# A tile of its own for one activation, quarter sums one product earlier, the first down page behind the additions, and a sum on VectorE

## The chip, the cores and the metric

The kernel runs on one core of a Trainium2 chip. The metric is the device time of one execution in microseconds (us); the time of a kernel is the median of its runs. The core has TensorE (PE, matmuls, with PEld for its weight loads), VectorE (DVE), ScalarE (ACT), GpSimd (POOL), and SyncE (SP), which here issues most of the DMAs.

## The reference

One layer of a hybrid encoder, for 1024 tokens of width 1024, in float32. Only its last part, the gated feed-forward network, is touched by the change.

```python
h = rmsnorm(x, norm1_g)
q, k, v, f_logit, u = split(h @ w_in)
x = x + concat(forgetting_attention(q, k, v, f_logit), multiscale_pool(u)) @ w_out
h2 = rmsnorm(x, norm2_g)                     # 1024 x 1024
gate, up = h2 @ w_gate, h2 @ w_up            # 1024 x 2816 each
x = x + (silu(gate) * up) @ w_down           # 1024 x 1024
return rmsnorm(x, final_g)
```

## The kernel before

**Precision.** Each float32 operand is split into a high part (rounded copy on ScalarE) and a low part (the difference, on VectorE). One product is three matmuls, high by high, low by high and high by low (`mm3`, lines 161 to 163). The split is `split` (lines 120 and 121). So a "page" of weights is ready for its first two matmuls when ScalarE is done, and for the third (L163) when VectorE is done.

**Gate and up.** The hidden width of 2816 is cut into 11 slices `j` of 256. The products of a slice with h2 are done in Strassen's (Winograd's) form, with seven products of half-size blocks instead of eight: P1 to P7. The blocks of h2 are fixed tiles (b11, b21, b22 and the sums t1 to t4, each with h and l). The weights of slice `j` are loaded as two raw tiles r0 and r1, GpSimd makes four sums of them (s1 to s4, lines 1070 to 1073), and the split of each operand is a page `gu{j}_P..`. The products add up in PSUM banks: c1 for P1, P6, P5 and P3 in turn, c2 for P2, c3 for P7 and P4. `snap` (L1135) copies a bank where its running sum is wanted later.

In slices 1 to 10 the third product, P3, is itself done in seven quarter products Q1 to Q7 (`fine_product`); the operands of h2 for these, sums and differences of quarters of b22, are made once, in slice 1, by the twelve steps of `fine_steps` (wholes at L1188, differences at L1195, splits at L121; the last split overwrites a quarter of b22h and b22l). Its weights come as two pages, P3a and P3b. After each quarter product VectorE adds it to a running sum (L1249); the seven share three PSUM regions (`fineA`, `fineB`, `fineC`), so some wait for such an addition. Slice 0 does P3 as one product.

**Features.** From the banks the four corners h11, h12, h21 and h22 of silu(gate) times up are made (`corner`): sums on VectorE (L1154, L1156) or none for h12 of slice 0 (L1151, L1152), the Silu on ScalarE (L1155), the multiplication on GpSimd (L1157). The value under the Silu lies in the tile `q`, of which there is one. GpSimd forms f1 to f4 of the corners (L1161), and all are written to memory (hsdP) for the down projection.

**Down.** It takes the slices in four groups `b` (2, 3, 3, 3 slices), each again in seven products (`ORDER2`). `down_raw` loads rows of w_down (r_wd), `down_sum` makes the four differences (L1312, tile `sum..`, shared by tag), `down_load` fetches the features back (r_f), and `down_page(i)` splits both into a page d0 to d3. After each product VectorE adds the four banks into rows of x (x2f, L1532), which have been reloaded; `gfb`, the final norm's weight, takes the place of tile `wmask`, in which the quarter operand of Q5 lies.

**What sets the order.** The program is written as a sequence; a scheduler then places the instructions on each engine's queue by its own estimate of when they can run, within what tiles and banks allow. `tc.issue_after(x)` keeps an instruction behind `x`. An engine works its queue strictly in order. The loop over `todo` (from line 1354) issues for each product the page two products ahead, the product, the corners due, and on the last slice the first steps of the down projection: `down_raw` after P1, two sums after P6, two loads after P7, and `down_page(0)` after P3a. `finer` holds the twelve quarter steps, of which three are issued after each product.

Of the kernel before, what the change touches and what calls it, by code (L numbers as in the profile page):

```python
# [45 lines left out]
def tile_kernel(  # L46
# [16 lines left out]
    nc = tc.nc  # L63
# [53 lines left out]
    mark = {}  # L117

    def split(hi, lo, src, eng=nc.vector):
        mark["hi"] = nc.scalar.activation(out=hi, in_=src, func=AF.Copy)  # L120
        return eng.tensor_tensor(out=lo, in0=src, in1=f32(hi), op=ALU.subtract)  # L121
# [789 lines left out]
    def blk_tile(key, shape, dt, name):  # L911
        pl, tag = (vpool, IN_V[key]) if key in IN_V else (blk, key)
        return pl.tile(shape, dt, tag=tag, bufs=1, name=name)
# [145 lines left out]
    def wk_tile(tag, bufs, name):  # L1059
        return wk.tile([P, 512], F32, tag=tag, bufs=bufs, name=name)  # L1060
# [79 lines left out]
    def feature(j, name, key):  # L1140
        t = feats[name] = wk_tile("h", 8, f"{name}_{j}")
        if key:
            spills.append((hsd[key, j], t))
        return t

    def corner(j, name, key, src, to):

        h = feature(j, name, to)
        q = wk_tile("q", 1, f"q{name}_{j}")
        if key is None:  # L1150
            nc.scalar.activation(out=q, in_=banks[src, 0], func=AF.Silu)  # L1151
            nc.vector.tensor_tensor(out=h, in0=banks[src, 1], in1=q, op=ALU.mult)  # L1152
        else:
            nc.vector.tensor_tensor(out=q, in0=banks[src, 0], in1=snaps[j, key, 0], op=ALU.add)  # L1154
            nc.scalar.activation(out=q, in_=q, func=AF.Silu)  # L1155
            nc.vector.tensor_tensor(out=h, in0=banks[src, 1], in1=snaps[j, key, 1], op=ALU.add)  # L1156
            nc.gpsimd.tensor_tensor(out=h, in0=h, in1=q, op=ALU.mult)  # L1157
# [93 lines left out]
    def spill(q=nc.scalar):  # L1251
        while spills:
            d, h = spills.pop(0)
            q.dma_start(out=d, in_=h)
# [53 lines left out]
    def down_sum(b, k):  # L1308
        a0, a1 = dict(P5=("b12", "P1"), P6=("P3", "P5"), P7=("P3", "b12"), P4=("P2", "P6"))[k]
        t = blk_tile(SUMS[k], [P, len(GROUPS[b]), 512], F32, f"sum{k}_{b}")  # L1310
        eng = nc.gpsimd if (b, k) in ((0, "P7"), (0, "P4"), (1, "P5")) else nc.vector
        eng.tensor_tensor(out=t, in0=moving[b, a0], in1=moving[b, a1], op=ALU.subtract)  # L1312
        moving[b, k] = t

# [13 lines left out]
    def down_page(i):  # L1328
        b, k = steps2[i]
        n = len(GROUPS[b])  # L1330
        fh, fl, wh, wl = (blk_tile(t, [P, n, 512], R, f"d{i}_{m}") for m, t in enumerate(PAGES[i % 2]))
        split(wh, wl, moving[b, k])
        split(fh, fl, raw2.pop(i))
        stationary[i] = fh, fl, wh, wl
# [19 lines left out]
    for i, (j, k) in enumerate(todo):  # L1354
        if i + 2 < len(todo):
            next_page(*todo[i + 2])
        if i:
            spill()
        if i == 1:
            product(j, k, 0, (0, 1))  # L1360
            with tc.issue_after(mark["turn", ORDER[-1]].ins):
                product(j, k, 0, (2, 3))
                product(j, k, 1)
        elif i and (k in ("P3a", "P3b") or k == "P4" and j):
            acc = [snaps[j, "sU4", n] for n in range(2)]
            pieces = dict(
                P3a=("Q1", "Q2", "Q7", (0, (0, 1)), (0, (2, 3)), "Q6", "Q4"), P4=((1, (0, 1)), "Q5", (1, (2, 3))),
                P3b=("Q3",),
            )
            for piece in pieces[k]:  # L1370
                with tc.issue_after(mark["mm"].ins):
                    if isinstance(piece, str):
                        fine_product(j, "P3", piece, acc)
                    else:
                        product(j, "P4", *piece)
        elif i:
            for n in range(2):
                product(j, k, n)
        if (j, k) == (NG - 1, "P3b"):
            last_features = lambda j=j, k=k: after(j, k)  # L1380
        else:
            after(j, k)
        if j == NG - 1:
            if k == "P1":
                for par in range(2):
                    down_raw(0, par)
            if k == "P6":
                for key in ("P5", "P6"):
                    down_sum(0, key)
            if k == "P7":  # L1390
                for par in range(2):
                    down_load(par)
            if k == "P3a":
                down_page(0)
        if j == 1 and k == "P2":
            finer += fine_steps("b22")
        for _ in range(min(3, len(finer))):
            finer.pop(0)()
        pages.pop((j, k))
# [10 lines left out]
    for k in ("P7", "P4"):  # L1410
        down_sum(0, k)
# [80 lines left out]
    for i, (b, k) in enumerate(steps2):  # L1492
# [3 lines left out]
        if b and k in ("P1", "P2", "P6"):  # L1496
            with tc.issue_after(added.ins):
                down_sum(b, dict(P1="P6", P2="P7", P6="P4")[k])
# [78 lines left out]
```

## Time and profile before

| | |
|---|---|
| median of 3 runs | 1045.78 us (1044.71 to 1046.29) |
| the profiled execution's own time | 1044.93 us |
| its span | 1043.2 us |
| mean granted TensorE clock | 0.995 |
| busy: PE, DVE, ACT, POOL | 98%, 69%, 45%, 39% of the span |
| matmuls (PE) | 5284 |

The profile is one execution. A row of the timeline gives start and duration in us, engine, line, operation, output and inputs, shape and count; in brackets stands the idle time of that engine just before and what ended it. Buffer numbers are left out of names: `gu_P_l` is the low part of any page. A row of windows gives for a stretch its length, the busy time of PE, PEld, DVE, ACT and POOL, the granted clock (1.00 is full), the DMA engines' busy share and GB/s. A duration of a row includes an overlap of some 0.08 us with the next instruction on the engine, so the step from one start to the next is a little shorter.

### The profile page before, as it was taken

To read this page: it belongs to the slowest core of one execution; us is meant where nothing else is said; L and a number is where in the kernel's file an instruction comes from. 1 tells how busy PE (TensorE), PEld (TensorE's weight loads), DVE (VectorE), ACT (ScalarE), POOL (GpSimd) and SP (SyncE) were. 2 spreads that over 40 slices of the span, in tenths; PEclk is the share of its full clock that TensorE was granted. 3 is DMA by queue.
4 is the path that set the end of the run, shared out by engine and by line. 5 is a ranking of instruction groups with operands and counts; after the bars stand their busy time and mean duration, and the time that the engine had idled before them with its cause. 6 is when DMAs were issued, how large, how long until landed. Compare 5 with 4: busy or idle time off the path is not lost.

```text
span 1043.2 us, 14702 instructions
## 1 busy us (share of the span) xinstructions
PE 1026.5 (98%) x5284; PEld 876.5 (84%) x5284; DVE 715.2 (69%) x1130; ACT 465.9 (45%) x747; POOL 410.6 (39%) x317
## 2 busy tenths in 40 slices
PE   9999999999999999999999999999999999999997
PEld 8988888998888888787888888888888778888885
DVE  7464566675986488776455556546548799888886
ACT  7334355655764266443343333333334343333346
POOL 4450121213444141538548457556658330000045
PEclk9999999999999999999999999999999999999999
DMA  7224425233832242333242233323326665352424
GB/s 249 53 57 138 100 78 123 63 103 85 289 123 90 66 151 71 102 117 115 71 142 102 70 132 112 91 101 111 101 101 242 212 241 172 122 194 99 151 91 162
DMA packets 108249, 130.25 MB, mean 125 GB/s; under 512 B 7368, under 2 KB 70352, under 8 KB 108176
## 3 DMA queue, kind: packets, MB, share of 16 engines
q1 hardware_dynamic: 96544, 108.18, 32.9%
q10 hardware_dynamic: 11072, 19.69, 4.9%
q0 software_dynamic: 560, 1.44, 0.4%
q8 instruction: 42, 0.69, 0.3%
q14 instruction: 31, 0.25, 0.1%
HBM read 86.29 MB, written 33.03 MB: 114 GB/s over the span
## 4 chain that ended last, share of the span: by engine, by line
PE 47%; DVE 5%; DMA 2%; issue 1%; ACT 0%; POOL 0%; POOLq 0%; ACTq 0%; DVEq 0%; SPq 0%
PE gu_P L162 9%; PE gu_P L161 9%; PE gu_P L163 9%; PE d L162 5%; PE d L163 5%; PE d L161 5%; DVE d L121 2%; DVE x2f_s L1532 1%; DMA x2f_s<-x2d 1%; DVE x2f_r L1532 1%; DMA r_wd<-in_w_down_dram 0%; DVE gu_P3a_l L121 0%; DMA gfb<-in_final_g_dram 0%; DVE s L1213 0%; DVE b22l L121 0%
## 5 line engine op out<-in xcount | busy, mean ns | idle before, releaser
L162 PE MATMUL d<-d,d 128*128 128x512 f32 (+1 forms) x308 | 119.4, 389 | 1.1 <-DVE d L121 1.1
L163 PE MATMUL d<-d,d 128*128 128x512 f32 (+1 forms) x308 | 119.1, 388 | 0.0
L629 POOL TENSOR_SCALAR p<-p,rr 128x128 f32<-128x128 f32 (+3 forms) x64 | 48.6, 763 | 176.0 <-DVE rr L628 138.1
L161 PE MATMUL d<-d,d 128*128 128x512 f32 x308 | 107.8, 388 | 0.0
L120 ACT ACTIVATE d<-r_f 128x1536 fp32r<-128x1536 f32 (+1 forms) x28 | 38.7, 1384 | 113.6 <-PE d L162 113.6
L1157 POOL TENSOR_TENSOR h<-h,qh 128x512 f32<-128x512 f32 x33 | 61.9, 1875 | 54.3 <-ACT qh L1155 29.9
L121 DVE TENSOR_TENSOR gu_P_l<-r,gu_P_h 128x1024 fp32r<-128x1024 f32 x32 | 52.6, 1647 | 31.0 <-ACT gu_P_h L120 31.0
L1070 POOL TENSOR_TENSOR s<-r 128x1024 f32<-128x1024 f32 x10 | 24.0, 2400 | 122.3 <-DMA r<-in_w_up_dram 62.7
L120 ACT ACTIVATE gu_P_h<-r 128x1024 fp32r<-128x1024 f32 x32 | 33.8, 1061 | 84.7 <-issue 40.8
L162 PEld LDWEIGHTS d<-d,d 128*128 128x128 f32 x308 | 57.8, 188 | 14.2 <-DVE d L121 2.3
L161 PEld LDWEIGHTS d<-d,d 128*128 128x128 f32 x308 | 57.8, 188 | 11.9
L163 PEld LDWEIGHTS d<-d,d 128*128 128x128 f32 x308 | 57.8, 188 | 11.9
L1437 POOL TENSOR_SCALAR sse<-sse 128x1 f32<-128x1 f32 x7 | 3.5, 494 | 155.3 <-ACT junk L1433 155.3
L121 DVE TENSOR_TENSOR gu_P_l<-s,gu_P_h 128x1024 fp32r<-128x1024 f32 (+1 forms) x38 | 51.6, 1365 | 18.9 <-ACT gu_P_h L120 18.8
L626 ACT ACTIVATE p<-p,mn 128x128 f32<-128x128 f32 (+3 forms) x64 | 49.4, 772 | 31.6 <-DVE mn L620 28.7
L648 DVE TENSOR_TENSOR tl<-tp,th 128x512 fp32r<-128x512 f32 (+1 forms) x80 | 49.5, 632 | 9.6 <-ACT th L647 8.6
L121 DVE TENSOR_TENSOR d<-r_f,d 128x1536 fp32r<-128x1536 f32 (+1 forms) x28 | 46.8, 1671 | 6.2 <-ACT d L120 6.2
L163 PE MATMUL qk<-hTh,l_qk 128*128 128x512 f32 x128 | 50.7, 396 | 0.0
L161 PE MATMUL qk<-hTh,h_qk 128*128 128x512 f32 x128 | 50.6, 395 | 0.0
L162 PE MATMUL qk<-hTl,h_qk 128*128 128x512 f32 x128 | 50.4, 394 | 0.0
L647 ACT ACTIVATE th<-tp 128x512 fp32r<-128x512 f32 (+1 forms) x80 | 42.5, 550 | 16.7 <-PE tp L643 13.9
L1532 DVE TENSOR_TENSOR x2f_s<-d,x2f_s 128x512 f32<-128x512 f32 x64 | 42.4, 682 | 10.6 <-PE d L163 10.6
(803 smaller groups left out, 3232.1 us busy)
## 6 DMA issues: line engine op xcount, KB each, us to landing
r_f<-hsdP SPq DMA_DIRECT2D x77, 256.0 KB
r_wd<-in_w_down_dram SPq DMA_DIRECT2D x22, 512.0 KB
r<-in_w_gate_dram SPq DMA_DIRECT2D x21, 512.0 KB
r<-in_w_up_dram SPq DMA_DIRECT2D x21, 512.0 KB
hsdP<-f ACTq DMA_DIRECT2D x40, 256.0 KB
s<-hi SPq DMA_DIRECT2D x64, 128.0 KB
hsdP<-h ACTq DMA_DIRECT2D x32, 256.0 KB
x<-in_x_dram SPq DMA_DIRECT2D x8, 512.0 KB
```

The lines of the kernel that those rows point to most:

```text
L120: mark["hi"] = nc.scalar.activation(out=hi, in_=src, func=AF.Copy)
L121: return eng.tensor_tensor(out=lo, in0=src, in1=f32(hi), op=ALU.subtract)
L161: nc.tensor.matmul(ps, lh, rh, start=start, stop=False, **kw)
L162: nc.tensor.matmul(ps, lh, rl, start=False, stop=False, **kw)
L163: mark["mm"] = nc.tensor.matmul(ps, ll, rh, start=False, stop=stop, **kw)
L626: nc.scalar.activation(out=pr[:, :n], in_=pr[:, :n], func=AF.Exp, scale=-1.0, bias=mn, accum_out=rs)
L629: nc.gpsimd.tensor_scalar(out=pr[:, :n], in0=pr[:, :n], scalar1=rr, scalar2=1.0, op0=ALU.mult, op1=ALU.mult)
L647: nc.scalar.activation(out=th[:, :w], in_=tp[:, :w], func=AF.Copy)
L648: nc.vector.tensor_tensor(out=tl[:, :w], in0=tp[:, :w], in1=f32(th[:, :w]), op=ALU.subtract)
L1070: g(out=s1, in0=a21, in1=a22, op=ALU.add)
L1157: nc.gpsimd.tensor_tensor(out=h, in0=h, in1=q, op=ALU.mult)
L1532: added = nc.vector.tensor_tensor(out=row, in0=ps, in1=row, op=ALU.add)
```

## The change

It has four edits. The corner without a running sum (h12 of slice 0) gets tile `e2` instead of `q`; `e2` is the tag of a quarter operand, made later. The twelve quarter steps begin after slice 1's P1 instead of its P2. The first down page is placed behind the addition that came last in the program when it is issued (`mark["add"]`). The difference P5 of the second group moves from GpSimd to VectorE.

```diff
     def corner(j, name, key, src, to):
 
         h = feature(j, name, to)
-        q = wk_tile("q", 1, f"q{name}_{j}")
+        q = wk_tile("q" if key else "e2", 1, f"q{name}_{j}")
         if key is None:
...
     def down_sum(b, k):
         a0, a1 = dict(P5=("b12", "P1"), P6=("P3", "P5"), P7=("P3", "b12"), P4=("P2", "P6"))[k]
         t = blk_tile(SUMS[k], [P, len(GROUPS[b]), 512], F32, f"sum{k}_{b}")
-        eng = nc.gpsimd if (b, k) in ((0, "P7"), (0, "P4"), (1, "P5")) else nc.vector
+        eng = nc.gpsimd if (b, k) in ((0, "P7"), (0, "P4")) else nc.vector
...
             if k == "P3a":
-                down_page(0)
-        if j == 1 and k == "P2":
+                with tc.issue_after(mark["add"].ins):
+                    down_page(0)
+        if j == 1 and k == "P1":
             finer += fine_steps("b22")
```

The scheduler answers these edits with other orders. PE at the beginning of slice 1, before (`gu1_P20` and `gu1_P21` are the two PSUM banks of P2, `gu1_P2_h` and `_l` its page):

```order
L161 MATMUL gu1_P20_5251<-b21h_4435,gu1_P2_h_5172 128x512
L162 MATMUL gu1_P20_5251<-b21l_4436,gu1_P2_h_5172 128x512
L161 MATMUL gu1_P21_5264<-b21h_4435,gu1_P2_h_5172 128x512
L162 MATMUL gu1_P21_5264<-b21l_4436,gu1_P2_h_5172 128x512
L163 MATMUL gu1_P20_5251<-b21h_4435,gu1_P2_l_5173 128x512
```

The same place in the changed kernel:

```order
L161 MATMUL gu1_P10_5217<-b11h_4433,gu1_P1_h_5133 128x512
L162 MATMUL gu1_P10_5217<-b11l_4434,gu1_P1_h_5133 128x512
L161 MATMUL gu1_P11_5230<-b11h_4433,gu1_P1_h_5133 128x512
L162 MATMUL gu1_P11_5230<-b11l_4434,gu1_P1_h_5133 128x512
L161 MATMUL gu1_P20_5261<-b21h_4435,gu1_P2_h_5172 128x512
L162 MATMUL gu1_P20_5261<-b21l_4436,gu1_P2_h_5172 128x512
L161 MATMUL gu1_P21_5274<-b21h_4435,gu1_P2_h_5172 128x512
L162 MATMUL gu1_P21_5274<-b21l_4436,gu1_P2_h_5172 128x512
L163 MATMUL gu1_P10_5217<-b11h_4433,gu1_P1_l_5134 128x512
```

P1 now stands ahead of P2, and eight matmuls instead of four stand ahead of the first that reads a low half. On VectorE the multiplication of h12 (L1152) has moved from behind the splits of P1, P2 and P6 to ahead of them.

VectorE in slice 1, before, from the third quarter difference on (`fine_b22..` are the quarter operands, `qh22` the first sum of corner h22, which reads P7's bank):

```order
L1195 TENSOR_TENSOR fine_b2211_5328<-fine_b2211_5328,fine_b2200_5288 128x512
L121 TENSOR_TENSOR gu1_P3a_l_5333<-s4_1_5095,gu1_P3a_h_5332 128x1024
L121 TENSOR_TENSOR fine1_b22_5283<-fine_b2200_5288,fine1_b22_5283 128x512
L121 TENSOR_TENSOR fine3l_b22_5287<-fine_b2201_5290,fine3h_b22_5286 128x512
L1213 TENSOR_TENSOR s4_1_5095<-s4_1_5095 128x256
L121 TENSOR_TENSOR fine2l_b22_5285<-fine_b2211_5328,fine2h_b22_5284 128x512
L1213 TENSOR_TENSOR s4_1_5095<-s4_1_5095 128x256 x2
L1154 TENSOR_TENSOR qh22_1_5406<-gu1_P70_5339,sn1_sU40_5401 128x512
L121 TENSOR_TENSOR gu1_P4_l_5371<-r1_1_5089,gu1_P4_h_5370 128x1024
L1249 TENSOR_TENSOR sn1_sU40_5401<-fineA_1P3_5432,sn1_sU40_5401 128x256
L121 TENSOR_TENSOR gu1_P3b_l_5420<-s4_1_5095,gu1_P3b_h_5419 128x768
L1156 TENSOR_TENSOR h22_1_5405<-gu1_P71_5352,sn1_sU41_5403 128x512
```

The same stretch in the changed kernel:

```order
L1195 TENSOR_TENSOR fine_b2211_5295<-fine_b2211_5295,fine_b2200_5252 128x512
L121 TENSOR_TENSOR fine3l_b22_5251<-fine_b2201_5254,fine3h_b22_5250 128x512
L1195 TENSOR_TENSOR fine_b2210_5370<-fine_b2210_5370,fine_b2211_5295 128x512
L121 TENSOR_TENSOR gu1_P3a_l_5338<-s4_1_5095,gu1_P3a_h_5337 128x1024
L121 TENSOR_TENSOR fine2l_b22_5249<-fine_b2211_5295,fine2h_b22_5248 128x512
L121 TENSOR_TENSOR b22l_4444<-fine_b2210_5370,b22h_4443 128x2x256
L1213 TENSOR_TENSOR s4_1_5095<-s4_1_5095 128x256 x3
L121 TENSOR_TENSOR gu1_P4_l_5376<-r1_1_5089,gu1_P4_h_5375 128x1024
L1154 TENSOR_TENSOR qh22_1_5411<-gu1_P70_5344,sn1_sU40_5406 128x512
L1249 TENSOR_TENSOR sn1_sU40_5406<-fineA_1P3_5432,sn1_sU40_5406 128x256
L121 TENSOR_TENSOR gu1_P3b_l_5420<-s4_1_5095,gu1_P3b_h_5419 128x768
L1156 TENSOR_TENSOR h22_1_5410<-gu1_P71_5357,sn1_sU41_5408 128x512
```

The fourth whole, its difference and the split of b22l now stand ahead of P4's split and of `qh22`, and these two have changed places.

VectorE in the last slice, before, from P4's split on (`d0_1` and `d0_3` are the low halves of the first down page):

```order
L121 TENSOR_TENSOR gu10_P4_l_8080<-r1_10_7771,gu10_P4_h_8079 128x1024
L121 TENSOR_TENSOR d0_1_8176<-r_f0_8073,d0_0_8175 128x1024
L1154 TENSOR_TENSOR qh22_10_8112<-gu10_P70_8047,sn10_sU40_8107 128x512
L1249 TENSOR_TENSOR sn10_sU40_8107<-fineA_10P3_8125,sn10_sU40_8107 128x256
L121 TENSOR_TENSOR gu10_P3b_l_8121<-s4_10_7818,gu10_P3b_h_8120 128x768
L1156 TENSOR_TENSOR h22_10_8111<-gu10_P71_8060,sn10_sU41_8109 128x512
L1249 TENSOR_TENSOR sn10_sU40_8107<-fineC_10P3_8133,sn10_sU40_8107 128x256
L121 TENSOR_TENSOR d0_3_8178<-r_wd0_0_7963,d0_2_8177 128x1024
L1249 TENSOR_TENSOR sn10_sU41_8109<-fineB_10P3_8141,sn10_sU41_8109 128x256
```

The changed kernel, from the addition that stands last in these rows on:

```order
L1249 TENSOR_TENSOR sn10_sU41_8109<-fineB_10P3_8141,sn10_sU41_8109 128x256
L1249 TENSOR_TENSOR sn10_sU41_8109<-fineA_10P3_8125,sn10_sU41_8109 128x256
L1249 TENSOR_TENSOR sn10_sU41_8109<-fineB_10P3_8141,sn10_sU41_8109 128x256
L121 TENSOR_TENSOR d0_3_8178<-r_wd0_0_7963,d0_2_8177 128x1024
L121 TENSOR_TENSOR d0_1_8176<-r_f0_8073,d0_0_8175 128x1024
L1249 TENSOR_TENSOR sn10_sU41_8109<-fineA_10P3_8125,sn10_sU41_8109 128x256
L1249 TENSOR_TENSOR sn10_sU40_8107<-fineA_10P3_8125,sn10_sU40_8107 128x256
```

Both splits of the page now stand behind five of the slice's seven additions and ahead of the last two.

## The prediction, made before the result was known

> **What bounds the kernel now.** I read the page first. TensorE is busy for all but a sliver, so only work that keeps it waiting, or slows its clock, can move the time.
>
> ```profile
> PE 1026.5 (98%) x5284; PEld 876.5 (84%) x5284; DVE 715.2 (69%) x1130; ACT 465.9 (45%) x747; POOL 410.6 (39%) x317
> ```
>
> Next the view of waits, for PE alone. Its columns are microseconds in all, times, longest. The four rows that matter lie in three places: where slice 1 of the gate and up products begins, in slice 1's quartered third product, and from the end of the last slice into the down projection.
>
> ```profile
> PE gu_P L163 <- DVE gu_P_l L121: 2.3, 1, 2.3
> PE fineB_10P L161 <- DVE sn_sU L1249: 2.1, 1, 2.1
> PE fineB_1P L162 <- DVE b22l L121: 1.7, 1, 1.7
> PE d L162 <- DVE d L121: 1.1, 2, 0.6
> ```
>
> The timeline of PE gives exact idle times (in brackets) and the first matmuls of slices 1, 2 and 3 (435.62, 479.10, 516.88):
>
> ```profile
> 435.62 0.39 PE L161 MATMUL gu_P<-b21h,gu_P_h 128*128 128x512 f32 x1
> 438.96 0.58 PE L163 MATMUL gu_P<-b21h,gu_P_l 128*128 128x512 f32 x1 [2.27 <-DVE gu_P_l L121]
> 474.94 0.39 PE L162 MATMUL fineB_1P<-b22l,gu_P3a_h 128*128 128x256 f32 x1 [1.73 <-DVE b22l L121]
> 479.10 0.39 PE L161 MATMUL gu_P<-b11h,gu_P_h 128*128 128x512 f32 x1
> 516.88 0.39 PE L161 MATMUL gu_P<-b11h,gu_P_h 128*128 128x512 f32 x1
> 817.47 0.38 PE L161 MATMUL fineB_10P<-b22h,gu_P3a_h 128*128 128x256 f32 x1 [2.09 <-DVE sn_sU L1249]
> 824.04 0.39 PE L161 MATMUL d<-d,d 128*128 128x512 f32 x1
> 853.24 0.50 PE L162 MATMUL d<-d,d 128*128 128x512 f32 x1 [0.64 <-DVE d L121]
> ```
>
> An undisturbed slice takes 516.88 − 479.10 = 37.78 (its 144 full and 42 half-wide matmuls are the time of 165, so 0.229 for a full one); slice 1 takes 43.48, so 5.70 is lost there, though its two waits are only 2.27 + 1.73 = 4.00. The rest is the clock. In these stretches the column PEclk (after the five engines) is the granted clock:
>
> ```profile
> 439.00:443.00 4.00, 4.00 (x11) 3.14 (x12) 3.47 (x3) 0.93 (x2) 4.00 (x2) 0.57 0.17 66
> 818.00:822.00 4.00, 4.00 (x17) 3.43 (x17) 0.42 (x1) 0.00 (x0) 0.00 (x0) 0.57 0.65 222
> 473.00:477.00 4.00, 2.27 (x13) 1.83 (x14) 2.79 (x4) 1.06 (x1) 4.00 (x2) 1.00 0.02 7
> ```
>
> After the waits of 2.27 and 2.09 the mean clock over 4 us is 0.57, which costs 4 × 0.43 = 1.7 each; after 1.73 it stays 1.00. So 4.00 + 1.70 = 5.70 closes slice 1. In all 2.27 + 1.7 + 1.73 + 2.09 + 1.7 + 1.1 = **10.6 us** can be won.
>
> The Trainium skill, "TensorE: Matmul & The Clock Gate" (section "What's actually happening"), lets the clock fall to half after an idle window of about 3.4 us; here it fell after 2.1, so the measurement decides. By the page's figure the two clock terms would not belong to the waits; that result is a rival below.
>
> **The activation's own tile (first wait).** One tile `q` serves all corners in turn, so each waits for GpSimd's product of the one before.
>
> ```profile
> 440.46 0.60 ACT L1151 ACTIVATE qh<-gu_P 128x512 f32<-128x512 f32 x1 [3.47 <-POOL h L1157]
> 441.09 0.69 DVE L1152 TENSOR_TENSOR h<-gu_P,qh 128x512 f32<-128x512 f32 x1
> 433.14 5.76 DVE L121 TENSOR_TENSOR gu_P_l<-r,gu_P_h 128x1024 fp32r<-128x1024 f32 x2 [1.85 <-ACT gu_P_h L120]
> ```
>
> Until 441.78 bank c1 (slice 0's P3) isn't free for slice 1's P1, so PE takes P2 (b21) first, whose low half is the second of the two splits at 433.14, done at 438.9. With its own tile the Silu needs only PE's P3, which ends before slice 0's last P4, and the multiplication goes ahead of the two splits. It costs DVE 0.69, which fits into the 1.85 idle before 433.14; on ScalarE the Silu's 0.60 lies in idle time ahead of the next DMA issue. P1 then runs first and P2's high parts are interleaved, so eight matmuls (8 × 0.229 = 1.8) run before the first low half is needed at 437.4. The first split ends at 433.14 + 2.9 = 436.0, the second at 438.9 against a need after 441.9. The term is −2.27 − 1.7 = **−3.97**; if the first split slips past 437.4, the term shrinks one for one (bound: −2.5, both splits needed).
>
> **Quarter sums one product earlier (second wait).** The last of them, b22l, ends at 474.88; PE's wait of 1.73 ended at 474.94, so it was wanted at 473.2.
>
> ```profile
> 449.58 0.69 DVE L1154 TENSOR_TENSOR qh<-gu_P,sn_sP 128x512 f32<-128x512 f32 x1 [1.19 <-POOL h L1157]
> 452.56 2.99 DVE L1188 TENSOR_TENSOR fine_b<-b22h,b22l 128x512 f32<-128x512 f32 x3
> 456.61 2.13 DVE L1195 TENSOR_TENSOR fine_b<-fine_b,fine_b 128x512 f32<-128x512 f32 x3
> 460.39 0.68 DVE L121 TENSOR_TENSOR fine3l_b<-fine_b,fine3h_b 128x512 fp32r<-128x512 f32 x1
> 465.40 1.23 DVE L121 TENSOR_TENSOR gu_P_l<-r,gu_P_h 128x1024 fp32r<-128x1024 f32 x1 [2.12 <-ACT gu_P_h L120]
> 472.80 2.08 DVE L121 TENSOR_TENSOR b22l<-fine_b,b22h 128x512 fp32r<-128x512 f32 x1 [0.70 <-ACT b22h L120]
> 461.93 0.75 DVE L1213 TENSOR_TENSOR s<-s 128x256 f32<-128x256 f32 x2
> 485.74 1.21 DVE L121 TENSOR_TENSOR gu_P_l<-s,gu_P_h 128x1024 fp32r<-128x1024 f32 x1
> 490.73 0.39 PE L161 MATMUL gu_P<-t2h,gu_P_h 128*128 128x512 f32 x1
> 450.00:470.00 20.00, 20.00 (x98) 16.95 (x97) 14.84 (x22) 9.62 (x14) 2.65 (x3) 1.00 0.21 71
> ```
>
> Nothing is added, but all twelve steps now stand ahead of P4's split. What is late next? The qh row at 449.58 waits for GpSimd's product of the corner before, which doesn't move, while PE stands 4 us earlier: five products after 435.62 its first quarter matmul comes near 463.0 (5 × 24 × 0.229), P4 behind three quarter products at 465.1. P4 adds to a bank that DVE's second qh has to read first. So from 449.58 DVE must do two qh and one h (0.6 each in the queue: 1.9), four wholes (4 × 1.0), four differences (2.8), four small splits (2.5), three page splits (3.5) and three short sums (1.1): 15.8, done at 465.4. ScalarE's halves are not waited for if each is ready in turn; GpSimd is busy only 2.65 of these 20 us (last column but three), so I take free durations. The bounds of a new wait are 0 (two wholes run free at 0.6) and 2.1 (each of a dozen hand-overs adds 0.15). P4's split also releases the load of slice 2's second raw tile, from which GpSimd makes the sum for P6: the split's end goes from 466.6 to about 464.8, 1.8 earlier, while PE is 5.7 earlier. P6's split now ends at 486.95, PE wants it two matmuls behind 490.73: a slack of 4.2 falls to 0.3, so nothing more is waited for there. I take 0.5. The term is −1.73 + 0.5 = **−1.2**.
>
> **First down page behind the additions (third wait).**
>
> ```profile
> 809.78 1.22 DVE L121 TENSOR_TENSOR d<-r_f,d 128x1024 fp32r<-128x1024 f32 x1
> 814.84 2.25 DVE L121 TENSOR_TENSOR d<-r_wd,d 128x1024 fp32r<-128x1024 f32 x1
> 817.00 0.41 DVE L1249 TENSOR_TENSOR sn_sU<-fineB_10P,sn_sU 128x256 f32<-128x256 f32 x1
> 822.14 0.42 DVE L1249 TENSOR_TENSOR sn_sU<-fineA_10P,sn_sU 128x256 f32<-128x256 f32 x1 [3.06 <-PE fineA_10P L163]
> ```
>
> The two splits (1.14 and 2.16 in the queue) stand ahead of the addition that PE waits for. Moved behind the fifth addition in the order, that addition ends 3.3 earlier, at 814.1, before PE's need at 817.47 − 2.09 = 815.4. Q4 (six half-wide matmuls, 0.7) and its addition end near 816.5, the two splits at 818.8, in the 3.06 that DVE now idles. What is queued behind them is the addition of Q5, ended by 819.2; PE wants it for Q3 after Q4, half of P4, Q5 and the rest of P4, 4.1 behind 815.4: 819.5. The page itself is needed a Q3 later, near 820.2. The term is −2.09 − 1.7 = **−3.8**; the bound is −2.1, if the splits take 2 us longer beside GpSimd and Q3 waits 1.7.
> SP is reordered too: gfb, which waits for Q5's matmuls (tile `wmask`), goes ahead of two r_f loads of the second group and one x2 row.
>
> ```profile
> 822.14 0.33 SPq L1404 DMA_DIRECT2D gfb<-in_final_g_dram  x1
> ```
>
> It comes 3.8 earlier with Q5, so these three are issued near 818.5; the first of them to be read, the x2 row, has its reader behind three down steps of 24 × 0.229 = 5.5, after 836. I cost it at 0; without that cover it is one load of 512 KB, about 3 us.
>
> **The sum on VectorE (fourth wait).**
>
> ```profile
> 844.01 1.21 DVE L121 TENSOR_TENSOR d<-sumP,d 128x1024 fp32r<-128x1024 f32 x1
> 847.72 4.39 POOL L1312 TENSOR_TENSOR sumP<-r_wd 128x1536 f32<-128x1536 f32 x1 [9.09 <-DVE x2f_s L1532]
> 848.67 4.52 DVE L121 TENSOR_TENSOR d<-sumP,d 128x1024 fp32r<-128x1024 f32 x1
> 865.90 1.74 DVE L1312 TENSOR_TENSOR sumP<-r_wd,sumP 128x1536 f32<-128x1536 f32 x1
> 840.90 1.28 SPq L1304 DMA_DIRECT2D r_wd<-in_w_down_dram  x3
> 840.00:850.00 10.00, 10.00 (x46) 8.29 (x45) 10.00 (x13) 4.02 (x4) 2.28 (x1) 1.00 0.94 347
> ```
>
> DVE is full here (10.00 of 10), and its split beside GpSimd's sum takes 4.52 instead of 1.21. The sum costs 1.74 on DVE, and takes 3.31 away: 1.57 saved, against waits of 0.64 and then 0.45 (the rest of 1.1). The term is **−1.1**. It must find its load landed: 1.5 MB from 840.90 at 347 GB/s ends near 845.4, or 847 beside its neighbour; DVE comes at 848.7, and both move about 4 earlier. Bounds: −1.1, and +1.5 if it waits.
>
> The Trainium skill, "SBUF — State Buffer" (the table whose row is "Run DVE + GpSimd concurrently"), says to schedule whichever is off the critical path, which speaks for leaving the sum on GpSimd. By the rows the split ends 1.1 after GpSimd's sum does, as if it waited for all of it, so the sum charges DVE either way, and 1.74 is the cheaper.
>
> **Sum.** −3.97 − 1.2 − 3.8 − 1.1 = −10.1. The profiled execution took 1044.93 (span 1043.2): 1034.8. It lies 0.85 under the median of 1045.78, from which the same sum gives 1035.7. I forecast **1035.3**.
>
> **Rivals.**
> *The wait comes back in slice 1 or 2.* DVE's hand-overs make P4, or slice 2's P6, 2.1 late instead of 0.5, and the clock halves: 1.6 + 1.7 = 3.3 lost, **1038.6**. For it: 15.8 of work for 15.5 of time. Against it: the one long idle time in DVE's rows there, 2.12, hung on ScalarE, whose own order also moves forward. Chance 0.17.
> *The DVE sum waits for its load, or DVE stays the bound after 830.* Nothing of 1.1 is won and 1.5 is added: **1037.9**. For it: DMA at 0.94. Chance 0.13.
> *The half clock doesn't belong to the waits.* Both stay: 3.4 less, **1038.7**. Against it: 1.00 in the untroubled slices, and both falls begin right behind a wait. The page on the clock gate cited above would give this time. Chance 0.04.
> *The tile doesn't change PE's order in effect*, since both splits are needed anyway: 4.0 less, **1039.3**. Against: each low half is an instruction of its own. Chance 0.05.
> *Slower.* The twelve quarter steps run beside GpSimd and each takes 2.08, like b22l, not 0.68: 12 × 1.4 = 16.8 late, ahead of the pages of P5, P3a and P4; PE loses about 16 + 1.7 against 10.6: **1052**. It decides from about 10 us of lateness, seven of the twelve steps. Against it: GpSimd is busy 2.65 of the 20 us there. Chance 0.04.
>
> **How the numbers follow.** Forecast 0.55; rivals 0.17, 0.13, 0.04, 0.05, 0.04; 0.02 for anything else. The range runs from 1033.8 (all of 10.6, from 1044.93, and 0.5 of scatter) to 1040.0, which takes in four rivals. The likeliest case alone: 1034 to 1037. A measurement of this kernel can tell 0.2% (2.1 us) from nothing: faster 0.91, same 0.04, slower 0.05.
>
> **What would show it.** Right: PE's first matmul of slice 1 reads b11, and no wait over 0.3 follows before slice 2, which starts 37.8 to 38.5 later; the clock is 1.00 from slice 1 to the end of the down projection; DVE's splits of 128x1024 in the down projection all stay near 1.2; down matmuls start about 9 earlier than 824. Wrong: a clock row of 0.57 anywhere there, a PE wait on a P4 or P6 page in slices 1 and 2, or DVE idle ahead of the moved sum with a DMA as releaser.

## The result, and the profile after

The changed kernel takes **1034.55 us** (median of 4 runs, 1034.12 to 1035.78) against 1045.24 for the kernel before, run beside it (4 runs, 1042.77 to 1046.29): a ratio of 0.9903, 95% interval 0.9883 to 0.9923. The prediction was 1035.3, between 1033.8 and 1040.0. Two repeats gave ratios of 0.9909 (0.9892 to 0.9927) and 0.9912 (0.9898 to 0.9925). One run of the kernel before, of 5882 us, was in a slow state and is left out of the first of these. The profiled execution took 1035.78, with a span of 1034.0 against 1043.2.

The page's busy times, and PE's waits of the changed kernel (microseconds in all, times, longest):

```profile
PE 1022.9 (99%) x5284; PEld 873.6 (84%) x5284; DVE 711.6 (69%) x1131; ACT 465.2 (45%) x747; POOL 405.4 (39%) x316
...
PE d L162 <- DVE d L121: 0.5, 1, 0.5
...
PE gu_P L163 <- DVE gu_P_l L121: 0.3, 1, 0.3
```

The waits of 2.3, 2.1 and 1.7 are gone. One of 0.5 is left of the 1.1 in the down projection, and one of 0.3 is new. The timeline of PE shows where (in brackets the idle time just before); the rows are the first matmuls of slices 1, 2 and 3, the new wait, the first down matmul, the old wait, and the last matmul:

```profile
436.82 0.39 PE L161 MATMUL gu_P<-b11h,gu_P_h 128*128 128x512 f32 x1
474.44 0.39 PE L161 MATMUL gu_P<-b11h,gu_P_h 128*128 128x512 f32 x1
481.51 0.50 PE L163 MATMUL gu_P<-b21h,gu_P_l 128*128 128x512 f32 x1 [0.27 <-DVE gu_P_l L121]
512.81 0.39 PE L161 MATMUL gu_P<-b11h,gu_P_h 128*128 128x512 f32 x1
815.76 0.40 PE L161 MATMUL d<-d,d 128*128 128x512 f32 x1
855.05 0.50 PE L162 MATMUL d<-d,d 128*128 128x512 f32 x1 [0.45 <-DVE d L121]
1026.33 0.28 PE L163 MATMUL dlast<-d,d 128*128 128x256 f32 x1
```

The last matmul before was this one:

```profile
1035.50 0.28 PE L163 MATMUL dlast<-d,d 128*128 128x256 f32 x1
```

From these rows and those of the prediction the span divides as follows (us):

| stretch | before | after | difference | predicted |
|---|---|---|---|---|
| start to slice 1 (untouched) | 435.62 | 436.82 | +1.20 | 0 |
| slice 1 | 43.48 | 37.62 | −5.86 | −5.17 (tile, quarter sums) |
| slice 2 to the first down matmul | 344.94 | 341.32 | −3.62 | −3.8 (first down page) |
| first to last down matmul | 211.46 | 210.57 | −0.89 | −1.1 (sum on VectorE) |
| behind it | 7.7 | 7.7 | 0 | 0 |

The first row is scatter: in the eleven profiles of the experiments, which leave this part unchanged too, slice 1 begins anywhere from 435.80 to 437.29. The changed stretches won 10.37 where 10.07 had been forecast. The third row is the sum of two things: slice 2 itself grew from 37.78 to 38.37, where the new wait is, and the rest of the stretch fell from 307.16 to 302.95, by 4.21. In the view by windows (length, the five engines, granted clock, DMA share, GB/s) the two places that had shown 0.57 now show 1.00:

```profile
436.00:440.00 4.00, 4.00 (x20) 3.30 (x19) 4.00 (x2) 1.06 (x1) 4.00 (x2) 1.00 0.00 0
440.00:444.00 4.00, 4.00 (x19) 3.34 (x18) 3.19 (x3) 0.71 (x2) 4.00 (x2) 1.00 0.17 66
814.00:818.00 4.00, 4.00 (x22) 3.40 (x21) 2.82 (x6) 2.75 (x4) 0.00 (x0) 1.00 0.87 231
```

VectorE's timeline shows the four edits at work: the multiplication of h12 ahead of the two splits (432.46), b22l and P4's split in time (462.87, 464.59), the page's two splits behind the fifth addition (811.75 to 813.23), and the sum (841.12):

```profile
432.46 0.68 DVE L1152 TENSOR_TENSOR h<-gu_P,qh 128x512 f32<-128x512 f32 x1
434.54 5.82 DVE L121 TENSOR_TENSOR gu_P_l<-r,gu_P_h 128x1024 fp32r<-128x1024 f32 x2 [1.40 <-ACT gu_P_h L120]
...
462.87 0.68 DVE L121 TENSOR_TENSOR b22l<-fine_b,b22h 128x512 fp32r<-128x512 f32 x1
...
464.59 1.22 DVE L121 TENSOR_TENSOR gu_P_l<-r,gu_P_h 128x1024 fp32r<-128x1024 f32 x1
...
811.75 0.42 DVE L1249 TENSOR_TENSOR sn_sU<-fineB_10P,sn_sU 128x256 f32<-128x256 f32 x1 [0.29 <-PE fineB_10P L163]
812.09 1.22 DVE L121 TENSOR_TENSOR d<-r_wd,d 128x1024 fp32r<-128x1024 f32 x1
813.23 1.22 DVE L121 TENSOR_TENSOR d<-r_f,d 128x1024 fp32r<-128x1024 f32 x1
...
841.12 1.76 DVE L1312 TENSOR_TENSOR sumP<-r_wd 128x1536 f32<-128x1536 f32 x1
```

One sign that the prediction named did not come: not all of VectorE's splits of 128x1024 in the down projection stayed near 1.2. Those at 818.63, 823.87 and 825.90 took 2.32, 2.11 and 2.31, beside GpSimd's last work on the features; PE waited for none of them.

So the sum of the forecast came out. The experiments ask whether its terms did: each edit alone, then the sum's place, then the clock.

### The profile page after: what moved, and what is told of

Its sections match the earlier page's. It is cut to its first block, busy times and chain, and to the rows that moved or that the text cites. A ratio compares the mean times of both kernels' runs of the same rounds, so it can differ in the third digit from the quotient of the medians.

```text
span 1034.0 us, 14701 instructions
## 1 busy us (share of the span) xinstructions
PE 1022.9 (99%) x5284; PEld 873.6 (84%) x5284; DVE 711.6 (69%) x1131; ACT 465.2 (45%) x747; POOL 405.4 (39%) x316
## 4 chain that ended last, share of the span: by engine, by line
PE 49%; DVE 2%; DMA 1%; issue 1%; POOL 1%; ACT 0%; SPq 0%; POOLq 0%; ACTq 0%; DVEq 0%
PE gu_P L163 9%; PE gu_P L162 9%; PE gu_P L161 9%; PE d L162 5%; PE d L163 5%; PE d L161 5%; DMA r_wd<-in_w_down_dram 1%; DVE d L121 1%; DVE x2f_s L1533 0%; DMA r<-in_w_up_dram 0%; POOL f L1161 0%; DMA hsdP<-f 0%; DVE gu_P_l L121 0%; POOL h L1157 0%; POOL hsdP L1254 0%
## 5 line engine op out<-in xcount | busy, mean ns | idle before, releaser
L1157 POOL TENSOR_TENSOR h<-h,qh 128x512 f32<-128x512 f32 x33 | 64.5, 1955 | 34.8 <-ACT qh L1155 26.9
L1155 ACT ACTIVATE qh<-qh 128x512 f32<-128x512 f32 x33 | 20.9, 632 | 64.6 <-POOL f L1161 32.6
```

## Experiments: each edit alone

The four kernels ran on one chip beside 24 runs of the kernel before (median 1044.25, from 1042.82 to 1046.98). They had 5, 8, 10 and 10 runs, in the order below. The gains are one minus the ratio, times 1044.25.

**The tile alone.**

```diff
-        q = wk_tile("q", 1, f"q{name}_{j}")
+        q = wk_tile("q" if key else "e2", 1, f"q{name}_{j}")
```

> The tile edit alone, put into the kernel before. Prediction's theory (the first wait belongs to the shared tile, and the half clock to the wait): slice 1 goes from 43.48 to 39.5 us, no wait of 2.27, no clock of 0.57 near its beginning, the wait of 1.73 on b22l stays; time 4.0 below the kernel before (1041.2). Rival, hand-on: VectorE's chain in slice 1 hangs on GpSimd's product at 449.58, which does not move, so b22l ends where it did and PE, 3.97 earlier, waits 5.7 for it instead of 1.73; slice 1 stays at 43.5 and the time at 1045. Between them lies a wait on b22l of 2 to 5 us.

Measured: 1040.8 (ratio 0.9962, 0.9949 to 0.9975), a gain of 3.97, by the interval 2.6 to 5.3. PE's timeline, slice 1's first matmul, the wait on b22l, and slice 2's first:

```profile
436.07 0.39 PE L161 MATMUL gu_P<-b11h,gu_P_h 128*128 128x512 f32 x1
470.78 0.39 PE L162 MATMUL fineB_1P<-b22l,gu_P3a_h 128*128 128x256 f32 x1 [1.62 <-DVE b22l L121]
474.98 0.39 PE L161 MATMUL gu_P<-b11h,gu_P_h 128*128 128x512 f32 x1
```

Slice 1 takes 38.91. The wait on b22l is 1.62, not 5.7: counted from slice 1's first matmul PE wants b22l 4.5 us earlier than before, and VectorE's chain came 4.6 earlier. The hand-on rival falls.

**The quarter steps after P1 alone.**

```diff
-        if j == 1 and k == "P2":
+        if j == 1 and k == "P1":
             finer += fine_steps("b22")
```

> The twelve quarter steps after P1 alone. Prediction's theory: the wait of 1.73 goes and nothing takes its place, since PE is not earlier than in the kernel before; slice 1 goes from 43.48 to 41.75, the wait of 2.27 and its half clock stay; time 1.7 below the kernel before. Rival, contention: the twelve steps beside GpSimd take 2.08 each, not 0.68, and PE waits for pages of P5, P3a or P4; slice 1 longer than 50. Rival, hand-on: P4's split or its bank is late instead, slice 1 stays near 43.5.

Measured: 1039.98 (ratio 0.9965, 0.9954 to 0.9977), a gain of 3.65, twice the 1.7 expected; by the interval it is 2.4 to 4.8. PE's timeline has the first wait, and slice 2 begins 39.77 after slice 1's first matmul at 437.29:

```profile
440.35 0.50 PE L163 MATMUL gu_P<-b21h,gu_P_l 128*128 128x512 f32 x1 [1.99 <-DVE gu_P_l L121]
477.06 0.39 PE L161 MATMUL gu_P<-b11h,gu_P_h 128*128 128x512 f32 x1
```

39.77 is an undisturbed slice and the wait: 37.78 + 1.99. The wait on b22l is gone with nothing in its place, so neither contention nor hand-on happened. But there is no half clock behind the wait of 1.99, although the prediction charged 1.7 to that wait. Why the gain is larger is taken up below, behind the probes of the clock.

**The first down page behind the additions alone.**

```diff
             if k == "P3a":
-                down_page(0)
+                with tc.issue_after(mark["add"].ins):
+                    down_page(0)
```

> The first down page behind the additions alone. Prediction's theory: the wait of 2.09 and the half clock behind it both go; from the first matmul of slice 2 to the first of the down projection 344.94 becomes 341.1 us; time 3.8 below the kernel before. Rival, the half clock does not belong to the wait: a clock of 0.57 over 4 us stays near 818, that stretch takes 342.85 and the time is 2.1 below. Rival, hand-on: the page's splits hold up the addition of Q5, and Q3 waits 1.7; the time is 2.1 below too, but with a wait on fineA at Q3.

Measured: 1040.54 (ratio 0.9967, 0.9957 to 0.9977), a gain of 3.45. Between slice 2 (480.70) and the first down matmul lie 340.72 us, with no wait and no half clock of their own: as expected, and neither rival. Its two other waits, and the clock behind each in windows laid on the places where the clock can change, showed something else:

```profile
439.61 0.50 PE L163 MATMUL gu_P<-b21h,gu_P_l 128*128 128x512 f32 x1 [2.49 <-DVE gu_P_l L121]
474.96 0.39 PE L162 MATMUL fineB_1P<-b22l,gu_P3a_h 128*128 128x256 f32 x1 [2.27 <-DVE b22l L121]
480.70 0.39 PE L161 MATMUL gu_P<-b11h,gu_P_h 128*128 128x512 f32 x1
821.42 0.40 PE L161 MATMUL d<-d,d 128*128 128x512 f32 x1
```

```profile
435.40:438.80 3.40, 1.72 (x8) 1.10 (x6) 3.40 (x2) 1.06 (x1) 3.40 (x2) 1.00 0.01 2
438.80:442.20 3.40, 2.59 (x11) 2.17 (x12) 3.40 (x3) 0.60 (x1) 3.40 (x2) 1.00 0.18 72
442.20:445.60 3.40, 3.40 (x16) 2.81 (x16) 2.46 (x4) 1.70 (x2) 3.32 (x3) 1.00 0.06 17
...
472.90:476.30 3.40, 1.34 (x8) 1.25 (x9) 2.76 (x3) 0.51 (x1) 3.40 (x2) 1.00 0.00 0
476.30:479.70 3.40, 3.40 (x12) 2.95 (x12) 1.78 (x2) 0.55 (x1) 3.40 (x2) 0.50 0.00 0
```

The longer wait, 2.49, left the clock at 1.00; the shorter one, 2.27, halved it. The longer lies across two windows, in which PE is idle for 1.68 and 0.81; the shorter lies nearly whole in one, idle for 2.06 (2.04 on the grid's exact edges).

**The sum on VectorE alone.**

```diff
-        eng = nc.gpsimd if (b, k) in ((0, "P7"), (0, "P4"), (1, "P5")) else nc.vector
+        eng = nc.gpsimd if (b, k) in ((0, "P7"), (0, "P4")) else nc.vector
```

> The sum of the second down group on VectorE alone. Prediction's theory: both waits of the down projection, 0.64 and 0.45, belong to GpSimd's sum and go; from the first down matmul to the last 211.46 becomes 210.4 us, and the split of 4.52 takes 1.2; time 1.1 below. Rival: the second wait belongs to VectorE's full queue at the first page of 128x1536 and stays, as the changed kernel's trace suggests (0.45 there); 210.8, time 0.6 below. Rival: the sum waits for its load of 1.5 MB, VectorE shows idle time ahead of it released by a DMA, nothing won.

Measured: 1043.19 (ratio 0.9991, 0.9981 to 1.0000), a gain of 0.94, by the interval 0 to 2.0. In its profile the down projection has no wait. But neither has it in the profiles of the tile alone and the page alone, where the sum is still GpSimd's. The page alone, GpSimd and then VectorE:

```profile
846.75 4.49 POOL L1312 TENSOR_TENSOR sumP<-r_wd 128x1536 f32<-128x1536 f32 x1 [10.14 <-DVE d L121]
```

```profile
845.51 1.21 DVE L121 TENSOR_TENSOR d<-r_f,d 128x1024 fp32r<-128x1024 f32 x1
846.64 1.21 DVE L121 TENSOR_TENSOR d<-sumP,d 128x1024 fp32r<-128x1024 f32 x1
850.17 2.15 DVE L121 TENSOR_TENSOR d<-r_f,d 128x1024 fp32r<-128x1024 f32 x1
```

Here the split of sumP started at 846.64, 0.11 ahead of GpSimd's sum, and took 1.21. The four additions from PSUM that follow it ran beside the sum undisturbed, from 847.8 to 850.2, and the next split ended at 852.32, 1.08 behind the sum's end. In the kernel before the split started 0.95 behind the sum and took 4.52, ending 1.08 behind it. So a split that starts while GpSimd's sum is running waits for its end; what the sum costs hangs on whether a split or the additions fall beside it. Six profiles of this case have the sum on GpSimd (before, tile alone, steps alone, page alone, and two below), and in all six it starts while a split is running on VectorE and ends 3.43 to 3.46 behind the start of VectorE's next instruction, as if it too had waited for that split. Where the next instruction is another split (four profiles), that split took 4.52 each time; where it is the additions from PSUM (two), they ran on. Which split is running when the sum can start is a matter of about a microsecond; in four of the six the profile names the sum's load as what it had waited for.

PE pays less than VectorE. From its first to its last down matmul it takes 209.71 to 209.85 in the profiles without a wait there (tile, page and sum alone), and 211.46 and 211.47 in the two where the split took 4.52 (before and steps alone).

## Experiments: where the sum belongs

Three kernels took up that question, each measured beside the changed kernel itself: the sum left on GpSimd, the changed kernel as it is, and the sum later on VectorE. The first two ran side by side:

> The changed kernel once more, beside the two below. Theory: waits in VectorE's work vary little from execution to execution, the clock's grid lies elsewhere each time; since no wait of over 1.6 us is left, the clock stays at 1.00 from slice 1 to the last matmul wherever the grid lies, and the time scatters less than that of the kernel before (1042.8 to 1047.0, 24 runs): 1034.1 to 1036. Rival: the scatter of the kernel before has another source, and this one scatters by 4 us too.

> The changed kernel with the sum of the second group left on GpSimd. Prediction's theory: the sum beside VectorE's split costs 1.1 on PE wherever it falls, so this is 0.6 to 1.1 slower than the changed kernel, with a split of 128x1024 of over 4 us and waits of 0.6 on L162. Rival, formed on the four single edits: only a split that starts while GpSimd's sum is running waits for the sum's end; four additions from PSUM do not wait. The load lands near 841.0, the split of sumP starts at 841.0 too and is ahead of the sum or behind it by 0.1 us. If ahead, the additions run beside the sum, the next split takes about 2.1, PE has no wait over 0.3 from 830 to 870 and the time is 0.45 below the changed kernel; if behind, 0.6 above.

```diff
-        eng = nc.gpsimd if (b, k) in ((0, "P7"), (0, "P4")) else nc.vector
+        eng = nc.gpsimd if (b, k) in ((0, "P7"), (0, "P4"), (1, "P5")) else nc.vector
```

Measured: the changed kernel 1035.76 (1035.03 to 1035.91); with the sum on GpSimd 1033.76, its runs being 1036.76, 1033.50, 1033.55 and 1033.97. Three of its four runs lie below every run of the changed kernel, the fourth above them all. So the fourth edit, taken back, mostly makes the other three faster, not slower; the two forecasts, 0.45 below the changed kernel and 0.6 above it, each name the side of one kind of run, and both are too small. The run of 1036.76 is the profiled one. GpSimd's row, VectorE's, and PE's:

```profile
840.23 3.94 POOL L1312 TENSOR_TENSOR sumP<-r_wd 128x1536 f32<-128x1536 f32 x1 [9.54 <-DMA r_wd<-in_w_down_dram]
```

```profile
839.61 1.21 DVE L121 TENSOR_TENSOR d<-r_f,d 128x1024 fp32r<-128x1024 f32 x1
840.74 4.52 DVE L121 TENSOR_TENSOR d<-sumP,d 128x1024 fp32r<-128x1024 f32 x1
```

```profile
845.31 0.50 PE L162 MATMUL d<-d,d 128*128 128x512 f32 x1 [1.42 <-DVE d L121]
```

The sum started while the first split ran; the second started 0.51 behind the sum, and took 4.52. With the sum on VectorE, the repeated profile of the changed kernel shows the other price, a wait for the load in VectorE's queue:

```profile
841.17 1.76 DVE L1312 TENSOR_TENSOR sumP<-r_wd 128x1536 f32<-128x1536 f32 x1 [0.78 <-DMA r_wd<-in_w_down_dram]
```

PE waits 0.69 and 0.49 there. VectorE idle ahead of the moved sum with a DMA as releaser was one of the prediction's signs of being wrong; the first profile of the changed kernel had not shown it. The sum is not read before the next sum (P6 of the second group), some 15 us later, which led to a third place for it:

```diff
+                if (b, k) == (1, "P1"):
+                    down_sum(b, "P5")
                 down_sum(b, dict(P1="P6", P2="P7", P6="P4")[k])
...
-            down_sum(b + 1, "P5")
+            if b:
+                down_sum(b + 1, "P5")
```

> The changed kernel with the second group's sum kept on VectorE but taken later: behind the first page of the second group, just ahead of the sum that reads it, instead of behind the first group's page of P5. Theory (formed on the repeated run): at its place in the changed kernel the sum waits up to 0.8 for its load and then delays two splits, which costs PE 0.45 to 1.2; at the later place its load has long landed, and PE's waits on L162 near 844 and 855 go, without a new one behind 858; the time is 0.5 to 1.2 below the changed kernel, about 1034.6 on the chip where that takes 1035.5, and it scatters less than the sum on GpSimd. Rival: VectorE is full from 815 to 870 and the wait only moves behind 858; no difference.

> The changed kernel again, beside the two others with the second group's sum elsewhere. Theory: 1034.1 to 1036, with the sum waiting 0.1 to 0.8 for its load in the profile and PE 0.4 to 1.2 on L162. Rival: the 2.0 us between this and the sum on GpSimd of the last call was scatter, and the three agree within 0.5 us.

> The changed kernel with the sum on GpSimd, again. Theory of luck: two kinds of execution, as in the last call (1033.5, 1033.6, 1034.0 and 1036.8): where VectorE's split starts ahead of GpSimd's sum, nothing is lost (about 1033.6), where it starts behind, the split takes over 4 us and PE waits 1.9 in all (about 1035.5 to 1036.8). The profile shows one of the two, in agreement with its own time. Rival: it is slower by 1.1 in every execution, as the prediction's term says.

Measured on one chip, beside 9 runs of the kernel before (1044.66):

| | median | runs | ratio to before (95%) |
|---|---|---|---|
| changed kernel | 1035.15 | 1034.43 to 1036.66 | 0.9912 (0.9898 to 0.9925) |
| sum on GpSimd | 1033.98 | 1033.80, 1033.83, 1034.14; 1036.51 | 0.9902 (0.9888 to 0.9916) |
| sum later on VectorE | 1034.03 | 1033.87 to 1034.23 | 0.9897 (0.9884 to 0.9911) |

The runs of the changed kernel and of the late sum do not overlap; the medians lie 1.12 apart. The profiles account for it: from PE's first to its last down matmul are 210.71 in the changed kernel here (the sum waited 0.16 for its load, PE 0.49) and 209.60 with the late sum. In the late sum's profile VectorE waits for no load, and PE has no wait in the down projection:

```profile
851.70 1.75 DVE L121 TENSOR_TENSOR d<-r_wd,d 128x1536 fp32r<-128x1536 f32 x1
853.36 1.88 DVE L1536 TENSOR_TENSOR x2f_r<-d,x2f_r 128x512 f32<-128x512 f32 x3
855.16 1.75 DVE L1312 TENSOR_TENSOR sumP<-r_wd 128x1536 f32<-128x1536 f32 x1
```

Its own theory held, with 1.1 in the forecast 0.5 to 1.2. Its four runs lie within 0.4 us, with the median of the sum on GpSimd and none of the longer runs that has. The sum on GpSimd shows two kinds of execution both times, six near 1033.8 and two near 1036.6, as the theory of luck says. Both profiled ones are of the slower kind; in both the stretch of down matmuls is 212.06 or 212.07, 2.2 to 2.5 longer than in the profiles without a wait there, and so most of the 2.8 that part the two kinds. The faster kind is known here by its time alone. That the profiled run was of the slower kind both times, and none of the six others, leaves another reading open: that taking the profile shifts the load. The profiles of the tile and the page alone, where the sum costs nothing, show that it need not.

Whether the changed kernel scatters less, as its forecast said, is not settled: its thirteen runs lie from 1034.12 to 1036.66, one end outside 1034.1 to 1036, and the 24 of the kernel before from 1042.82 to 1046.98, but few runs spread less than many. Nor do the 24 times go with the granted clock: the five runs with a mean clock of 0.994 took 1043.6 to 1044.4, the four with 0.997 took 1042.8 to 1045.1.

## Experiments: what halves the clock

Two probes put a delay into VectorE's queue ahead of the addition that PE waits for, in slices 2 to 9 of the changed kernel.

```diff
+            if q == "Q7":
+                for _ in range(HOLD.get(j, 0)):
+                    nc.vector.tensor_tensor(out=out, in0=out, in1=out, op=ALU.max)
             mark["add"] = nc.vector.tensor_tensor(out=out, in0=ps, in1=out, op=ALU.add)
```

> The changed kernel with repeated maxima of the running sum with itself (it stays as it is) on VectorE ahead of Q7's addition in slices 2 to 9, 9 to 17 of them, so that PE waits about 1 to 4 us once in each slice. Window theory: the clock is decided on a fixed grid of 3.413 us, and falls to half for one such window behind a window in which PE was idle for more than about half of it (the six traces: 2.04 fell, 1.66 did not); so waits under 1.7 never fall, waits of 2.0 to 3.4 fall only where one window holds enough of them, waits over 3.9 always do. Rival, length: every wait over 2.0 falls, wherever it lies. Rival, whole window: only a window without any matmul falls, so no wait under 3.4 does.

The delays came out far longer than meant: ten of these maxima, which read and write only SBUF, took 13.09 beside GpSimd's sums, so PE waited 11 to 14 us each time. All eight waits halved the clock, on which the three theories agree. The second probe reads PSUM instead, and ten of its operations took 4.54 at the same place (a row of each probe, then the edit):

```profile
555.44 13.09 DVE L1253 TENSOR_TENSOR sn_sU<-sn_sU 128x256 f32<-128x256 f32 x10
```

```profile
546.27 4.54 DVE L1253 SCALAR_TENSOR_TENSOR sn_sU<-fineB_3P,sn_sU 128x256 f32<-128x256 f32 x10
```

```diff
-                    nc.vector.tensor_tensor(out=out, in0=out, in1=out, op=ALU.max)
+                    nc.vector.scalar_tensor_tensor(
+                        out=out, in0=ps, scalar=0.0, in1=out, op0=ALU.mult, op1=ALU.add
+                    )
```

> As the first probe of the clock, but the delay is made of 9 to 16 operations that read Q7's bank, multiply by zero and add the running sum (it stays as it is), so that none of them waits for GpSimd and each takes about 0.35. PE should wait between 1 and 4 us in each of slices 2 to 9. Window theory: half clock exactly behind each window of the 3.413 grid that holds more than 1.75 to 2.04 us of PE's idle time; so waits of 2.1 to 3.4 that lie across a window's edge, with under 1.75 on each side, leave the clock at 1.00. Length theory: every wait above 2.0 brings it. Whole window: none under 3.4 does.

Now PE waited 1.87, 2.33, 2.79, 3.25, 3.71, 4.17, 4.63 and 5.08. Three of these waits, in PE's timeline, and the windows of the clock's grid around the first, second and fourth:

```profile
509.61 0.39 PE L161 MATMUL fineB_2P<-b22h,gu_P3a_h 128*128 128x256 f32 x1 [1.87 <-DVE sn_sU L1256]
...
551.32 0.38 PE L161 MATMUL fineB_3P<-b22h,gu_P3a_h 128*128 128x256 f32 x1 [2.33 <-DVE sn_sU L1256]
...
636.30 0.39 PE L161 MATMUL fineB_5P<-b22h,gu_P3a_h 128*128 128x256 f32 x1 [3.25 <-DVE sn_sU L1256]
```

```profile
507.90:511.30 3.40, 1.69 (x10) 1.56 (x11) 2.31 (x6) 0.00 (x0) 3.40 (x3) 1.00 0.02 5
511.30:514.70 3.40, 3.40 (x19) 2.72 (x18) 0.83 (x1) 1.81 (x2) 3.32 (x3) 1.00 0.20 77
...
548.90:552.30 3.40, 1.07 (x8) 0.98 (x8) 2.53 (x7) 0.04 (x1) 3.40 (x3) 1.00 0.00 0
552.30:555.70 3.40, 3.40 (x12) 2.81 (x12) 1.96 (x2) 1.02 (x1) 3.32 (x2) 0.50 0.20 77
...
630.80:634.20 3.40, 2.25 (x13) 1.79 (x11) 3.16 (x8) 0.00 (x0) 3.38 (x2) 1.00 0.00 0
634.20:637.60 3.40, 1.30 (x9) 1.21 (x10) 2.53 (x7) 0.30 (x1) 3.40 (x3) 1.00 0.00 0
637.60:641.00 3.40, 3.40 (x13) 2.92 (x12) 0.14 (x1) 0.76 (x1) 3.32 (x2) 0.50 0.20 77
```

PE busy for 1.69 of a window leaves the next at 1.00; busy for 1.07 or 1.30, the next is at 0.50. The wait of 3.25 has 1.15 in one window and 2.10 in the next, and only the second halves the clock. The clock's records in the traces give the grid: the two falls of the kernel before lie 378.88 us apart, 111 times 3.413, and in every trace of this case the clock's changes lie whole numbers of these apart. Sorted by the part of a wait that lies in one window:

| kernel | wait | of it in one window, us | next window |
|---|---|---|---|
| before | 2.27; 1.73; 2.09 | 2.27; 1.58; 2.09 | half; full; half |
| tile alone | 1.62; 2.10 | 1.62; 2.10 | full; half |
| steps alone | 1.99; 2.10 | 1.05; 1.41 | full; full |
| page alone | 2.49; 2.27 | 1.66; 2.04 | full; half |
| sum alone | 1.85; 2.40; 2.09 | 1.15; 2.06; 1.58 | full; half; full |
| second probe | 1.87; 2.33; 2.79; 3.25 | 1.70; 2.33; 2.34; 2.10 | full; half; half; half |

In every case 1.70 or less left the clock alone and 2.04 or more halved it; the probe's four longer waits each have 2.05 or more in one window, and all halved it. The length theory falls by the waits of 2.09, 2.10 and 2.49 that halved nothing, the whole-window theory by 2.04. The window theory stands.

## Why the prediction was right, and where it wasn't

**The activation's own tile (−3.97): right, with a chance in it.** P1 comes first, PE's first matmul of slice 1 reads b11, and no low half is late. The wait and its half clock went, 3.97 by the single edit; with an interval of 2.6 to 5.3, that it agrees to the hundredth is luck. But the 1.7 of clock did not belong to the wait as such: a wait of 2.3 halves the clock only where over about 1.9 of it falls into one window. If the wait lies anywhere with equal chance, that happens in (3.41 + 2.3 − 2 × 1.9) / 3.41 = 0.56 of executions, an estimate. The profiled execution was one of these at both places.

**Quarter sums one product earlier (−1.73 + 0.5): mechanism right, size too small.** The step that failed is the 1.73, with no clock to it. It was read from an execution in which the first wait had halved the clock, which made PE slower on its way to b22l. Where that didn't happen (page alone, sum alone) the wait on b22l was 2.27 and 2.40, with a half clock behind it each time. The edit alone won 3.65, and the granted clock that is on record for every run bears out where it came from: its mean is 0.9973 over the eight runs of this edit alone and 0.9955 over the 24 of the kernel before. That is 0.0018 of 1044 or about 1.9 us, an estimate, which with a wait of 1.7 to 2.4 makes 3.6 to 4.3. In company with the tile less is left, as 1.62 in the tile-alone kernel shows. The loss of 0.5 was sized well and misplaced: PE waits 0.27 to 0.49 in six profiles, of the changed kernel and of those with the sum elsewhere, but on P2's low half in slice 2, not on P4's or P6's page; slice 2 takes 38.37 instead of 37.78. The upper bound of 2.1, with 0.15 for each hand-over between engines, a figure read from no row, was not reached.

**First down page behind the additions (−3.8): right.** The splits took 1.22 each in VectorE's idle time, and Q3 did not wait for the addition of Q5 behind them. The reordered loads cost nothing. The half clock here, too, was one execution's: with the same wait of 2.09 or 2.10 it fell in the kernel before and with the tile alone, and stayed in those of the steps and the sum alone. The gain over all runs is 3.45. In the profile of the page alone the stretch behind slice 2 fell by 4.2, 0.4 more than the wait and its clock; where the 0.4 comes from stays open.

**The sum on VectorE (−1.1): wrong sign in this company.** What failed is the sentence that the sum charges VectorE either way. Only a split that starts while GpSimd's sum runs is charged; additions from PSUM are not. On GpSimd the sum costs VectorE 3.3 or nothing, by which instruction falls beside it. On VectorE it always costs 1.7 of a full queue, and up to 0.78 more where its load is late, which was the rival of 0.13. The second wait, of 0.45 to 0.5 near 855, stayed with the sum at this place; with the sum later it went too, so here it belonged to the 1.7 in VectorE's queue. Alone the edit won 0.94; beside the others its medians lie 1.2 and 2.0 above those of the sum on GpSimd.

**The total.** The single gains add up to 3.97 + 3.65 + 3.45 + 0.94 = 12.0; together they gave 10.1, 9.5 and 9.2 in three comparisons. The fourth edit's change of sign, about 2.1 to 2.9, is enough to cover the difference; whether tile and quarter sums also overlap was not separated from it. The clock came out nearly right in sum, with its places wrong: 3.4 had been charged, at two waits, and the mean granted clock of the changed kernel in its two repeats (0.9988 and 0.9982, against 0.9948 and 0.9947) is worth 4.1 and 3.7 us. By the table above a half clock came behind either of the two waits in only some of the executions, and behind a third, the one on b22l, in others. That the forecast of 1035.3 lay so close owes something to two errors of opposite sign: the quarter sums were worth more than charged, the sum less.

**Rivals.** The slower one, contention of the quarter steps with GpSimd, did not occur: in the changed kernel b22l took 0.68 instead of 2.08. The one with a wait back in slice 1 or 2 came at a small size only, 0.27 to 0.49 without a half clock. That the tile changes nothing, and that the clock doesn't belong to waits at all, fell with the tile alone and with the probe.

## What to carry to other kernels

A cost that one profile shows behind a wait may be that execution's: before charging a half clock to a wait, look at how the wait lies on the clock's windows, and at the mean granted clock of the other runs (0.994 to 0.997 in 24 runs of the kernel before, 0.998 or 0.999 in all thirteen of the changed one). For work that two engines could do, ask which instruction starts while the other runs, not how much each has to do; and ask when the result is first read, since a place 15 us later was as fast here as the better kind of run on the other engine, without the worse kind.

## What the runs showed of the hardware

- The clock is decided on a free grid of 3.413 us: half for one window behind each window with 2.04 us or more of PE idle, full behind each with 1.74 or less (the 1.74 is from the first probe). At half clock, in the same probe, a window with 0.56 idle was followed by full clock, one with 1.14 was not. The Trainium skill, "TensorE: Matmul & The Clock Gate" (section "What's actually happening"), calls the window free-running, of 3413 ns; the traces agree. It speaks of an idle window; here one that was 60% idle was enough.
- Ten VectorE operations that touch only SBUF took 13.09 beside GpSimd's sums; ten of another kind that read PSUM took 4.5 at the same place. A split that started 0.05 or 0.11 ahead of GpSimd's sum was not delayed; one that started 0.10 to 0.95 behind it took 4.52 and ended 1.1 after it. GpSimd's sum of 128x1536 was recorded at 3.53 to 4.54, and ended about 3.4 behind the split that was running when it started.
